# Gates of the gathered experts: one-number indirect transfers in place of a key comparison per slot, compaction ahead of the gate matrix

## The chip, the core and the metric

The kernel runs on one core of a Trainium2 chip. Times are microseconds (us) on the device, of one launch. The engines named below are PE (matrix products), DVE (vector), ACT (activation and copies out of PSUM), POOL (here it issues the indirect transfers) and SP (issues the plain transfers).

## The reference, cut to what matters

One encoder layer over 256 tokens of width 2048: a mixer, a cross attention, and a PEER feed-forward in which every token picks 8 x 16 = 128 of 16384 one-neuron experts. Only the last part is touched:

```python
eid  = (i1 * PEER_N_KEYS + i2).reshape(t, PEER_HEADS * PEER_TOPK)
gate = jax.nn.softmax(top_sc, axis=-1).reshape(t, PEER_HEADS * PEER_TOPK)
u = u_tab[eb]
act = jax.nn.gelu(jnp.einsum('td,tkd->tk', xb, u).astype(jnp.float32))
return jnp.einsum('tk,tkd->td', (gb * act).astype(xb.dtype), v_tab[eb])
```

## The kernel before, in words

The expert tables are rearranged on the host into 128 rows of 128 experts. 104 rows (`RD`) are done densely: products of all their experts with all tokens (the U stage, `u_chunk`, 13 chunks of which the first 6, `LEAD`, run ahead), a multiplication by a gate matrix (`prep`), and products with the second table (the V stage, `v_chunk`, into which the other 7 U chunks are mixed). The experts of the other 24 rows are gathered: each token has at most 40 (`NIT`) of them in slots, and for each slot POOL fetches one row per token (`rows`, 128 x 2048 floats, four buffers in a ring), DVE makes the dot product (`dot`, result `junk`) and later adds the row of the second table times its coefficient (`axpy`, result `hh`). There are 2 token tiles (`tt`) of 128 tokens, 5 blocks of 8 slots each, so 80 dots and 80 axpys.

Every weight of the dense part is loaded as `raw` (128 x 1024, four buffers), rounded by ACT to `hi`, and DVE makes the remainder `lo` (L112, three buffers). PE uses both. A DVE that is late with `lo` stops PE.

`route` (L671) finds the experts and gates of a tile. `gbuild` (L768) writes the gate matrix: for 4 tokens at a time DVE makes two one-hot tiles (L777, L780), ACT scales one (L783), PE multiplies them (`G`, L793), ACT copies the result (L795), and every 16 tokens go to memory (`gd`). `compact` (L753) sorts the gathered slots to the front: five rounds of `pick` (L745, L746) on a key per slot, then `rows_of` (L748) makes the table rows `idx`. The key also holds the slot's place j in its low 7 bits. `weigh` (L891) finds the gates of 8 picked slots: for each slot one comparison of the 128 keys with the picked key, times the masked gates `gsp`, summed along the row (L895).

These side programs are generators. `Weave.pump` takes steps of the first in the list while it has credit, each pump of the main loop adds `rate`, and each `yield` says what a step costs. In `chosen` a block's `weigh` costs 1.8, each dot or axpy 2.2; the rate in the V stage is 1.25 (`RC`). In the sixth U chunk (L848) the rest of `gbuild` is pumped out at once. What this emits is a priority: a list scheduler then sets each engine's order, and each engine works in that fixed order.

Of the kernel before, what the change touches and what calls it, by code (L numbers as in the profile page):

```python
# [21 lines left out]
TT = T // P  # L22
# [11 lines left out]
RD = 104  # L34
# [3 lines left out]
NIT = 40  # L38
# [29 lines left out]
def hybrid_layer_kernel(ctx: ExitStack, tc: tile.TileContext, a: dict, out: bass.AP, dbg=None):  # L68
    nc = tc.nc
# [10 lines left out]
    wv = Weave()  # L80
# [19 lines left out]
    ones = cp.tile([P, P], F32, name="ones")  # L100

# [152 lines left out]
    nc.sync.dma_start(iota, a["iota"])  # L254
    for b in range(1, 8):
        if b == 3:
            wv.add(prep_x())
        col_block(a["w_xyg"], b, xT, xb[:, b, :])
# [409 lines left out]
    i1T, rT, gtT, key, work, gsp, sel, idx = ({} for _ in range(8))  # L668
    flag = cp.tile([P, TT], F32, name="flag")

    def route():  # L671
# [11 lines left out]
        for tt in range(TT):  # L683
# [41 lines left out]
            for j, src in enumerate((i1, rr, gt.rearrange("p h j -> p (h j)"))):  # L725
# [4 lines left out]
            key[tt] = tp.tile([P, P], F32, tag=f"key{tt}", name="key")  # L730
            work[tt] = tp.tile([P, P], F32, tag=f"work{tt}", name="work")
            gsp[tt] = tp.tile([P, P], F32, tag=f"gsp{tt}", name="gsp")
            V.scalar_tensor_tensor(gsp[tt], rr, float(RD), gt.rearrange("p h j -> p (h j)"),
                                   op0=ALU.is_ge, op1=ALU.mult)
            V.tensor_scalar(rr, rr, float(P * P), -float(RD * P * P), op0=ALU.mult, op1=ALU.add)
            V.scalar_tensor_tensor(rr, i1, float(P), rr, op0=ALU.mult, op1=ALU.add)
            V.tensor_tensor(key[tt], rr, iota, op=ALU.add)
            V.tensor_copy(work[tt], key[tt])
# [9 lines left out]
    def rows_of(tt, s):  # L748
        V.tensor_copy(idx[tt][:, s], sel[tt][:, s])
        V.tensor_scalar(idx[tt][:, s].bitcast(U32), idx[tt][:, s].bitcast(U32), 7, None,  # L750
                        op0=ALU.logical_shift_right)

    def compact():  # L753
        for tt in range(TT):
            sel[tt] = tp.tile([P, NIT + 8], F32, tag=f"sel{tt}", name="sel")
            idx[tt] = tp.tile([P, NIT], I32, tag=f"idx{tt}", name="idx")
            for b in range(NB):
                pick(tt, b)
                yield 0.4
            V.max(sel[tt][:, NIT:], work[tt])  # L760
            V.tensor_scalar(flag[:, tt:tt + 1], sel[tt][:, NIT:NIT + 1], 0.0, None, op0=ALU.is_ge)
            rows_of(tt, slice(0, NIT))
            yield 0.6
# [125 lines left out]
    dots, coef, gsel = {}, {}, {}  # L889

    def weigh(tt, b):  # L891
        gsel[tt, b] = tp.tile([P, 8], F32, tag="gsel", name="gsel", bufs=3)
        for k in range(8):
            gj = tp.tile([P, P], F32, tag="gj", name="gj")
            V.scalar_tensor_tensor(gj, key[tt], sel[tt][:, 8 * b + k:8 * b + k + 1], gsp[tt],  # L895
                                   op0=ALU.is_equal, op1=ALU.mult, accum_out=gsel[tt, b][:, k:k + 1])

    def dot(tt, b, k, gat):
        if k == 0:
            dots[tt, b] = tp.tile([P, 8], F32, tag="dots", name="dots", bufs=2)  # L900
        V.scalar_tensor_tensor(junk, gat, 1.0, h[tt], op0=ALU.mult, op1=ALU.mult,  # L901
                               accum_out=dots[tt, b][:, k:k + 1])
        if k == 7:
            c = coef[tt, b] = tp.tile([P, 8], F32, tag="coef", name="coef", bufs=3)
            A.activation(c, dots[tt, b], AF.Gelu_apprx_tanh)
            V.tensor_tensor(c, c, gsel[tt, b], op=ALU.mult)
# [4 lines left out]
    def chosen(blocks):  # L911
# [8 lines left out]
        for n in range(len(tasks) + AHEAD):  # L920
# [11 lines left out]
    def rest():  # L932
# [7 lines left out]
        with tc.If(left > 0):  # L940
            for tt in range(TT):
                for b in range(NB, P // 8):
                    pick(tt, 0)
                    rows_of(tt, slice(0, 8))
# [70 lines left out]
    done.add("pb")  # L1015
    wv.add(gbuild())
    wv.add(compact())
# [53 lines left out]
def _constants():  # L1071
# [13 lines left out]
    return {"cs": np.ascontiguousarray(cs), "md": np.ascontiguousarray(md), "iota": iota,  # L1085
            "ident": np.eye(P, dtype=np.float32)}
# [51 lines left out]
```

## Time and profile before

| | us |
|---|---|
| median of 3 runs | 2260.44 |
| lowest, highest | 2258.86, 2264.28 |
| the profiled execution's own time | 2268.65 |
| its span, first to last instruction | 2266.9 |

| engine | busy us | share of the span |
|---|---|---|
| PE | 2142.0 | 94% |
| DVE | 1812.3 | 80% |
| ACT | 1084.5 | 48% |
| POOL | 397.1 | 18% |

The U stage's first six chunks lie at about 920 to 1260 us, the V stage after that, the last chunk and the output from about 2200 us. PE is busy nearly all the time everywhere but around 1250 us, DVE above all in `route` (900 to 1110 us) and in the V stage. A share is a mean over stages, so what a stage is bound by is read from the stage.

### The profile page before, as it was taken

To read this page: it belongs to the slowest core of one execution; us is meant where nothing else is said; L and a number is where in the kernel's file an instruction comes from. 1 tells how busy PE (TensorE), PEld (TensorE's weight loads), DVE (VectorE), ACT (ScalarE), POOL (GpSimd) and SP (SyncE) were. 2 spreads that over 40 slices of the span, in tenths; PEclk is the share of its full clock that TensorE was granted. 3 is DMA by queue.
4 is the path that set the end of the run, shared out by engine and by line. 5 is a ranking of instruction groups with operands and counts; after the bars stand their busy time and mean duration, and the time that the engine had idled before them with its cause. 6 is when DMAs were issued, how large, how long until landed. Compare 5 with 4: busy or idle time off the path is not lost.

```text
span 2266.9 us, 30039 instructions
## 1 busy us (share of the span) xinstructions
PE 2142.0 (94%) x10830; PEld 1795.0 (79%) x10830; DVE 1812.3 (80%) x2511; ACT 1084.5 (48%) x1639; POOL 397.1 (18%) x218
## 2 busy tenths in 40 slices
PE   8999989999999999999998799999989999898898
PEld 7787878888888888888997577877878777776676
DVE  6748876545544579999978799999989989999985
ACT  6564435444444455545887343434434343443334
POOL 0303120000000000000001222323333232243501
PEclk9999999999999999999999899999999999999999
DMA  8664645565544575556765999977777998876664
GB/s 276 235 211 155 216 132 173 176 191 183 184 141 141 176 241 167 186 179 222 225 200 184 368 343 362 324 250 268 226 283 255 371 336 323 291 267 200 191 212 142
DMA packets 162824, 521.65 MB, mean 230 GB/s; under 512 B 23572, under 2 KB 52756, under 8 KB 149268
## 3 DMA queue, kind: packets, MB, share of 16 engines
q1 hardware_dynamic: 139632, 419.29, 56.2%
q0 software_dynamic: 23040, 100.41, 11.8%
q8 instruction: 85, 1.39, 0.2%
q14 instruction: 67, 0.55, 0.1%
HBM read 569.19 MB, written 17.83 MB: 259 GB/s over the span
## 4 chain that ended last, share of the span: by engine, by line
PE 57%; DVE 15%; issue 12%; DMA 11%; POOL 3%; ACT 2%; POOLq 0%; DVEq 0%; ACTq 0%; SPq 0%
PE U L121 8%; PE wb L121 7%; DVE lo L112 6%; PE xc L160 5%; PE xc L159 5%; PE xc L161 5%; PE U L124 4%; PE wb L124 4%; PE V L860 4%; PE V L861 4%; PE V L859 4%; POOL gat L884 2%; DMA gat<-in_Us_dram,idx 2%; PE G L793 2%; DMA raw<-in_V_dram 2%
## 5 line engine op out<-in xcount | busy, mean ns | idle before, releaser
L111 ACT CAST hi<-raw 128x1024 fp32r<-128x1024 f32 x700 | 734.4, 1050 | 780.5 <-DMA raw<-in_V_dram 255.5
L112 DVE TENSOR_TENSOR lo<-raw,hi 128x1024 fp32r<-128x1024 f32 x700 | 862.0, 1249 | 277.0 <-PE xc L160 140.8
L121 PE MATMUL U<-xn,hi 128*128 128x512 f32 x1664 | 414.2, 397 | 16.4 <-ACT hi L111 16.4
L121 PEld LDWEIGHTS U<-xn,hi 128*128 128x128 f32 x1664 | 308.0, 191 | 75.6 <-ACT hi L111 17.2
L884 POOL DMA_INDIRECT gat<-in_Us_dram,idx x80 | 124.2, 1553 | 1129.1 <-PE U L121 677.3
L124 PE MATMUL U<-xn,lo 128*128 128x256 f32 x1664 | 230.9, 287 | 24.4 <-DVE lo L112 24.1
L860 PE MATMUL V<-lo,ah 128*128 128x512 f32 x560 | 225.7, 403 | 24.2 <-DVE lo L112 23.7
L124 PEld LDWEIGHTS U<-xn,lo 128*128 128x128 f32 x1664 | 217.4, 192 | 38.2 <-DVE lo L112 30.3
L884 POOL DMA_INDIRECT gat<-in_Vs_dram,idx x80 | 185.0, 2312 | 337.1 <-DVE hh L909 304.5
L861 PE MATMUL V<-hi,al 128*128 128x512 f32 x560 | 223.0, 398 | 0.0
L859 PE MATMUL V<-hi,ah 128*128 128x512 f32 x560 | 221.0, 398 | 1.7 <-ACT hi L111 1.5
L901 DVE SCALAR_TENSOR_TENSOR junk<-gat,h 128x2048 f32<-128x2048 f32 x80 | 183.7, 2296 | 14.6 <-DMA gat<-in_Us_dram,idx 14.6
L909 DVE SCALAR_TENSOR_TENSOR hh<-gat,coef,hh 128x2048 f32<-128x2048 f32 x80 | 187.9, 2349 | 5.1 <-DMA gat<-in_Vs_dram,idx 5.1
L860 PEld LDWEIGHTS V<-lo,ah 128*128 128x128 f32 x560 | 106.2, 190 | 59.1 <-DVE lo L112 33.4
L859 PEld LDWEIGHTS V<-hi,ah 128*128 128x128 f32 x560 | 106.1, 189 | 28.8 <-ACT hi L111 2.4
L861 PEld LDWEIGHTS V<-hi,al 128*128 128x128 f32 x560 | 106.2, 190 | 24.9
L860 PE MATMUL V<-lo,xe 128*128 128x512 f32 x256 | 103.1, 403 | 14.1 <-DVE lo L112 14.1
L121 PE MATMUL wb<-hT,hi 128*128 128x512 f32 x448 | 113.9, 398 | 0.7 <-ACT hi L111 0.7
L861 PE MATMUL V<-hi,xe 128*128 128x512 f32 x256 | 101.3, 396 | 0.0
L859 PE MATMUL V<-hi,xe 128*128 128x512 f32 x256 | 96.2, 394 | 3.8 <-ACT hi L111 3.8
L121 PEld LDWEIGHTS wb<-hT,hi 128*128 128x128 f32 x448 | 81.3, 189 | 16.3 <-ACT hi L111 0.9
L121 PE MATMUL wb<-xT,hi 128*128 128x512 f32 x368 | 91.7, 400 | 0.2 <-ACT hi L111 0.2
(330 smaller groups left out, 3234.6 us busy)
## 6 DMA issues: line engine op xcount, KB each, us to landing
raw<-in_U_dram SPq DMA_DIRECT2D x208, 512.0 KB, 4.8
raw<-in_V_dram SPq DMA_DIRECT2D x208, 512.0 KB, 4.4
raw<-in_w_xyg_dram SPq DMA_DIRECT2D x48, 512.0 KB, 4.7
raw<-in_w_qkv_dram SPq DMA_DIRECT2D x48, 512.0 KB, 4.2
raw<-in_w_xk_dram SPq DMA_DIRECT2D x32, 512.0 KB, 4.4
raw<-in_w_xv_dram SPq DMA_DIRECT2D x32, 512.0 KB, 4.4
raw<-in_w_out_dram SPq DMA_DIRECT2D x32, 512.0 KB, 4.0
raw<-in_w_xq_dram SPq DMA_DIRECT2D x32, 512.0 KB, 4.5
```

Source lines behind the costliest of these rows:

```text
L111: A.copy(hi, raw)
L112: V.tensor_tensor(lo, raw, hi.bitcast(F32), op=ALU.subtract)
L121: PE.matmul(pt, hi[:, k * P:(k + 1) * P], xt[:, kb, :], start=(kb == 0), stop=(kb == KB - 1))
L124: PE.matmul(pt[:, :T], lo[:, k * P:(k + 1) * P], xt[:, kb, :T], start=False, stop=False)
L159: PE.matmul(pt, xh, hi[:, w], start=(n == 0), stop=False)
L160: PE.matmul(pt, xh, lo[:, w], start=False, stop=False)
L859: PE.matmul(pt, ah[:, c, t_], hi[:, w], start=(c == 0), stop=False)
L860: PE.matmul(pt, ah[:, c, t_], lo[:, w], start=False, stop=False)
L861: PE.matmul(pt, al[:, c, t_], hi[:, w], start=False, stop=(c == 7))
L884: G.indirect_dma_start(gat, None, a[tab], bass.IndirectOffsetOnAxis(ap=idx[tt][:, k:k + 1], axis=0), bounds_check=NS - 1, oob_is_err=False)
L901: V.scalar_tensor_tensor(junk, gat, 1.0, h[tt], op0=ALU.mult, op1=ALU.mult, accum_out=dots[tt, b][:, k:k + 1])
L909: V.scalar_tensor_tensor(hh[tt], gat, coef[tt, b][:, k:k + 1], hh[tt], op0=ALU.mult, op1=ALU.add)
```

## The change

The gates of a tile are written to memory (`gtd`, 16384 numbers). `compact` is now ahead of `gbuild` in the list. After the five picks, `rows_of` takes the place j from the key's low bits, adds 128 times the token's lane (a new constant `lane`, loaded at the start), and so has an index tile `at` into `gtd`. 40 indirect transfers per tile then fetch one number for each of the 128 tokens into a column of `gsel`. `weigh`, `gsp` and the separate `key` go. In place of the mask in `gsp`, one small operation per block (`g8`) takes the slots with a key of at least 0.

```diff
+    gtd = [dp.tile([P * P, 1], F32, name=f"gtd{tt}") for tt in range(TT)]
...
-            key[tt] = tp.tile([P, P], F32, tag=f"key{tt}", name="key")
+            nc.sync.dma_start(gtd[tt].rearrange("(p j) o -> p (j o)", p=P), gt.rearrange("p h j -> p (h j)"))
...
-            V.scalar_tensor_tensor(gsp[tt], rr, float(RD), gt.rearrange("p h j -> p (h j)"),
-                                   op0=ALU.is_ge, op1=ALU.mult)
...
-            V.tensor_tensor(key[tt], rr, iota, op=ALU.add)
-            V.tensor_copy(work[tt], key[tt])
+            V.tensor_tensor(work[tt], rr, iota, op=ALU.add)
...
     def rows_of(tt, s):
         V.tensor_copy(idx[tt][:, s], sel[tt][:, s])
+        at = tp.tile([P, NIT + 8], I32, tag="at", name="at")[:, s]
+        V.tensor_scalar(at, idx[tt][:, s], P - 1, None, op0=ALU.bitwise_and)
         V.tensor_scalar(idx[tt][:, s].bitcast(U32), idx[tt][:, s].bitcast(U32), 7, None,
                         op0=ALU.logical_shift_right)
+        V.tensor_scalar(at, at, lane, None, op0=ALU.add)
+        for k in range(s.start, s.stop):
+            G.indirect_dma_start(gsel[tt][:, k:k + 1], None, gtd[tt], bass.IndirectOffsetOnAxis(
+                ap=at[:, k - s.start:k - s.start + 1], axis=0), bounds_check=P * P - 1, oob_is_err=False)
+            yield 0.05
...
-            rows_of(tt, slice(0, NIT))
+            gsel[tt] = tp.tile([P, NIT + 8], F32, tag=f"gsel{tt}", name="gsel")
+            yield from rows_of(tt, slice(0, NIT))
...
-    def weigh(tt, b):
-        gsel[tt, b] = tp.tile([P, 8], F32, tag="gsel", name="gsel", bufs=3)
-        for k in range(8):
-            gj = tp.tile([P, P], F32, tag="gj", name="gj")
-            V.scalar_tensor_tensor(gj, key[tt], sel[tt][:, 8 * b + k:8 * b + k + 1], gsp[tt],
-                                   op0=ALU.is_equal, op1=ALU.mult, accum_out=gsel[tt, b][:, k:k + 1])
...
-            V.tensor_tensor(c, c, gsel[tt, b], op=ALU.mult)
+            g8 = tp.tile([P, 8], F32, tag="g8", name="g8")
+            V.scalar_tensor_tensor(g8, sel[tt][:, 8 * b:8 * b + 8], 0.0, gsel[tt][:, 8 * b:8 * b + 8],
+                                   op0=ALU.is_ge, op1=ALU.mult)
+            V.tensor_tensor(c, c, g8, op=ALU.mult)
...
-                if f is dot and k == 0:
-                    weigh(tt, b)
-                    yield 1.8
...
     done.add("pb")
+    wv.add(compact())
     wv.add(gbuild())
-    wv.add(compact())
```

The orders below have no time in them. DVE, the end of the second tile's picks before (the names in brackets are the semaphores that a row waits for; DMASW are those of the indirect transfers, DMAHW of the plain ones):

```order
L745 MAX sel<-work 128x8 [waits DVE_49]
L895 SCALAR_TENSOR_TENSOR gj,gsel<-key,sel,gsp 128x128 [waits DVE_49]
L746 MATCH_REPLACE work<-sel,work 128x128 [waits DVE_49]
L749 CAST idx<-sel 128x40
L895 SCALAR_TENSOR_TENSOR gj,gsel<-key,sel,gsp 128x128 [waits DVE_49]
L112 TENSOR_TENSOR lo<-raw,hi 128x1024 [waits DMAHW1_49,PE_49,Activation_49]
```

and the same place after the change:

```order
L745 MATCH_REPLACE work<-sel,work 128x128 [waits DVE_49]
L748 CAST idx<-sel 128x40
L766 MAX sel<-work 128x8 [waits DVE_49]
L750 TENSOR_SCALAR at<-idx 128x40 [waits DMASW4_49,DMASW3_49,DMASW5_49,DMASW2_49,DMASW6_49,DMASW1_49,DMASW7_49,DMASW0_49,DVE_49]
L767 TENSOR_SCALAR flag<-sel 128x1 [waits DVE_49]
L751 TENSOR_SCALAR idx<-idx 128x40 [waits DVE_49]
L753 TENSOR_SCALAR at<-at,lane 128x40
L113 TENSOR_TENSOR lo<-raw,hi 128x1024 [waits DMAHW2_49,PE_49,Activation_49]
```

The `at` tile has one buffer for both token tiles, so the second tile's `at` row waits for the indirect transfers that read the first tile's; the program's count for each of the eight semaphores there is five transfers, which is all 40, and `lo` rows stand behind it. Between the first tile's last `at` row and this one DVE has 14 `lo` rows.

POOL, its first indirect transfers before:

```order
L884 DMA gat_11170<-in_Us_dram,idx 128x2048
L884 DMA gat_11171<-in_Us_dram,idx 128x2048
L884 DMA gat_11172<-in_Us_dram,idx 128x2048
L884 DMA gat_11173<-in_Us_dram,idx 128x2048
L884 DMA gat_11170<-in_Us_dram,idx 128x2048
```

and after:

```order
L755 DMA gsel<-gtd_6493,at 128x1 x40
L891 DMA gat_11416<-in_Us_dram,idx 128x2048
L891 DMA gat_11417<-in_Us_dram,idx 128x2048
L891 DMA gat_11418<-in_Us_dram,idx 128x2048
L755 DMA gsel<-gtd_6494,at 128x1 x40
L891 DMA gat_11419<-in_Us_dram,idx 128x2048
```

The first tile's 40 stand ahead of all rows of the expert table, the second tile's 40 behind the first three of them.

PE, the end of the gate matrix before (a group of 4 `G` products is 4 tokens):

```order
L124 MATMUL U<-xn,lo 128x256 x2
L793 MATMUL G<-o_10795,o_10793 128x104 x4
L793 MATMUL G<-o_10809,o_10807 128x104 x4
L793 MATMUL G<-o_10824,o_10822 128x104 x4
L793 MATMUL G<-o_10839,o_10837 128x104 x4
L793 MATMUL G<-o_10853,o_10851 128x104 x4
L124 MATMUL U<-xn,lo 128x256 x8
```

and after, the last 11 of its 12 groups that stand without a `U` product between them:

```order
L800 MATMUL G<-o_10986,o_10984 128x104 x4
L800 MATMUL G<-o_11001,o_10999 128x104 x4
L800 MATMUL G<-o_11015,o_11013 128x104 x4
L800 MATMUL G<-o_11029,o_11027 128x104 x4
L800 MATMUL G<-o_11044,o_11042 128x104 x4
L800 MATMUL G<-o_11059,o_11057 128x104 x4
L800 MATMUL G<-o_11073,o_11071 128x104 x4
L800 MATMUL G<-o_11087,o_11085 128x104 x4
L800 MATMUL G<-o_11102,o_11100 128x104 x4
L800 MATMUL G<-o_11117,o_11115 128x104 x4
L800 MATMUL G<-o_11131,o_11129 128x104 x4
L125 MATMUL U<-xn,lo 128x256 x8
```

Seven groups have moved from places among `U` products to this end; the place in the row of `U` products is the same.

## Rows read from the trace of the kernel before

**Rows 1.** Busy us of each engine in five stretches, granted clock, DMA share.

```profile
core 0: us, PE busy (x) PEld busy (x) DVE busy (x) ACT busy (x) POOL busy (x), PEclk, DMA share, GB/s
1047.50:1084.50 37.00, 36.67 (x215) 32.12 (x214) 35.70 (x68) 17.78 (x28) 4.71 (x3) 1.00 0.70 246
1236.00:1260.00 24.00, 4.49 (x16) 3.65 (x16) 14.21 (x12) 4.75 (x9) 7.99 (x4) 0.64 0.99 349
1260.00:1280.00 20.00, 19.71 (x95) 16.64 (x96) 18.61 (x20) 9.98 (x14) 4.82 (x4) 0.92 0.94 353
1300.00:2000.00 700.00, 654.23 (x3171) 539.35 (x3170) 642.45 (x651) 289.96 (x363) 214.90 (x117) 0.99 0.84 303
2000.00:2200.00 200.00, 182.06 (x763) 143.70 (x763) 195.59 (x177) 74.57 (x74) 70.01 (x29) 0.98 0.66 210
```

**Rows 2.** Waits between 1300 and 2200 us: us in total, times, longest.

```profile
PE V L860 <- DVE lo L112: 37.5, 31, 3.7
...
PE U L124 <- DVE lo L112: 20.4, 17, 2.2
```

**Rows 3.** DVE groups, 1200 to 2266 us: busy, mean ns, idle before.

```profile
L895 DVE SCALAR_TENSOR_TENSOR gj<-key,sel,gsp 128x128 f32<-128x128 f32 x56 | 19.4, 347 | 0.0
...
L895 DVE DVE_READ_ACCUMULATOR gj<-key,sel,gsp 128x1 f32 x56 | 4.6, 82 | 0.0
...
L906 DVE TENSOR_TENSOR coef<-coef,gsel 128x8 f32<-128x8 f32 x10 | 1.6, 162 | 0.0
```

**Rows 4.** Timeline of POOL, its first gathers: start, us taken, idle before.

```profile
1061.94 1.16 POOL L884 DMA_INDIRECT gat<-in_Us_dram,idx  x1 [673.28 <-PE U L121]
1067.07 1.74 POOL L884 DMA_INDIRECT gat<-in_Us_dram,idx  x1 [3.97 <-PE U L121]
1082.53 1.82 POOL L884 DMA_INDIRECT gat<-in_Us_dram,idx  x1 [13.73 <-DVE sel L745]
1238.25 2.00 POOL L884 DMA_INDIRECT gat<-in_Us_dram,idx  x1 [153.90 <-DVE gat L1031]
```

**Rows 5.** DVE groups, 1047.5 to 1084.5 us.

```profile
L112 DVE TENSOR_TENSOR lo<-raw,hi 128x1024 fp32r<-128x1024 f32 x13 | 15.5, 1209 | 0.0
L1031 DVE MEMSET gat<- 128x2048 f32 x3 | 5.3, 1765 | 1.1 <-issue 1.1
```

**Rows 6.** Instructions of line 884: ns min/median/max.

```profile
L884 POOL DMA_INDIRECT gat<-in_Us_dram,idx x80: 984/1670/4308, 1061.9 to 2115.3; - x80
...
DMA to landing us min/median/max: 2.1/7.4/10.3
```

**Rows 7.** Timeline of DVE, then of POOL, around 1980 us.

```profile
1979.45 2.23 DVE L811 TENSOR_TENSOR act<-raw,act 128x1024 f32<-128x1024 f32 x1
1981.59 2.35 DVE L112 TENSOR_TENSOR lo<-raw,hi 128x1024 fp32r<-128x1024 f32 x2
1983.86 2.29 DVE L901 SCALAR_TENSOR_TENSOR junk<-gat,h 128x2048 f32<-128x2048 f32 x1
...
1987.21 0.68 DVE L873 TENSOR_TENSOR hh<-hh,V 128x512 f32<-128x512 f32 x1
...
1979.80 8.35 POOL L884 DMA_INDIRECT gat<-in_Vs_dram,idx  x1 [4.69 <-DVE hh L909]
1988.46 1.44 POOL L884 DMA_INDIRECT gat<-in_Us_dram,idx  x1 [0.30 <-issue]
```

**Rows 8.** Timeline of PE, last groups of G.

```profile
1229.97 1.29 PE L793 MATMUL G<-o,o 128*128 128x104 f32 x8 [0.32 <-ACT o L783]
...
1234.44 1.28 PE L793 MATMUL G<-o,o 128*128 128x104 f32 x8 [0.20 <-ACT o L783]
```

**Rows 9.** Chain of waits, 1195 to 1290 us: start, us, what.

```profile
1199.30 1.77 PE G L793 x16
...
1236.29 11.39 DMA gd<-gs
...
1247.77 8.43 DMA raw<-gd
```

More of the change, by code (lines that the diff above doesn't have):

```diff
@@ L100, in hybrid_layer_kernel @@
     ones = cp.tile([P, P], F32, name="ones")
+    lane = cp.tile([P, 1], F32, name="lane")
     def raw_tile(src):
@@ L254, in hybrid_layer_kernel @@
     nc.sync.dma_start(iota, a["iota"])
+    nc.sync.dma_start(lane, a["lane"])
     for b in range(1, 8):
@@ L666, in top16 @@
                 V.match_replace(src, vals[:, rs], src, -3.0e38)
-    i1T, rT, gtT, key, work, gsp, sel, idx = ({} for _ in range(8))
+    i1T, rT, gtT, work, sel, idx, gsel = ({} for _ in range(7))
+    gtd = [dp.tile([P * P, 1], F32, name=f"gtd{tt}") for tt in range(TT)]
     flag = cp.tile([P, TT], F32, name="flag")
@@ L729, in route @@
             i1T[tt], rT[tt], gtT[tt] = trio[:, 0], trio[:, 1], trio[:, 2]
-            key[tt] = tp.tile([P, P], F32, tag=f"key{tt}", name="key")
+            nc.sync.dma_start(gtd[tt].rearrange("(p j) o -> p (j o)", p=P), gt.rearrange("p h j -> p (h j)"))
             work[tt] = tp.tile([P, P], F32, tag=f"work{tt}", name="work")
-            gsp[tt] = tp.tile([P, P], F32, tag=f"gsp{tt}", name="gsp")
-            V.scalar_tensor_tensor(gsp[tt], rr, float(RD), gt.rearrange("p h j -> p (h j)"),
-                                   op0=ALU.is_ge, op1=ALU.mult)
             V.tensor_scalar(rr, rr, float(P * P), -float(RD * P * P), op0=ALU.mult, op1=ALU.add)
             V.scalar_tensor_tensor(rr, i1, float(P), rr, op0=ALU.mult, op1=ALU.add)
-            V.tensor_tensor(key[tt], rr, iota, op=ALU.add)
-            V.tensor_copy(work[tt], key[tt])
+            V.tensor_tensor(work[tt], rr, iota, op=ALU.add)
             yield 2.5
@@ L888, in hybrid_layer_kernel @@
     turn = [0]
-    dots, coef, gsel = {}, {}, {}
-    def weigh(tt, b):
-        gsel[tt, b] = tp.tile([P, 8], F32, tag="gsel", name="gsel", bufs=3)
-        for k in range(8):
-            gj = tp.tile([P, P], F32, tag="gj", name="gj")
-            V.scalar_tensor_tensor(gj, key[tt], sel[tt][:, 8 * b + k:8 * b + k + 1], gsp[tt],
-                                   op0=ALU.is_equal, op1=ALU.mult, accum_out=gsel[tt, b][:, k:k + 1])
+    dots, coef = {}, {}
     def dot(tt, b, k, gat):
@@ L943, in rest @@
                     pick(tt, 0)
-                    rows_of(tt, slice(0, 8))
+                    for _ in rows_of(tt, slice(0, 8)):
+                        pass
                     for _ in chosen([(tt, 0)]):
@@ L1085, in _constants @@
     return {"cs": np.ascontiguousarray(cs), "md": np.ascontiguousarray(md), "iota": iota,
+            "lane": np.arange(P, dtype=np.float32).reshape(P, 1) * P,
             "ident": np.eye(P, dtype=np.float32)}
```

## The prediction

> **What bounds the kernel now.** Read first the table of busy time by stretch [rows 1]: its rows give, for each stretch, how long each engine worked. From 1047.5 to 1084.5 us, in the U stage, PE works 36.67 of 37.00 us and DVE 35.70: both are full, PE sets the pace, and DVE only just keeps up. From 1236 to 1260 us PE works 4.49 of 24 us. That gap is not an engine's: the chain of waits shows the last piece of the gate matrix written to memory in 11.39 us and read back in 8.43 us [rows 9]. From 1300 to 2200 us PE works 654.23 + 182.06 = 836 of 900 us and DVE 642.45 + 195.59 = 838. Read next what PE waits for there [rows 2]: of its 64 idle us, 37.5 + 20.4 = 57.9 ended with a `lo` from DVE. So in the V stage less DVE work can help, in the U stage it cannot, and whatever stops DVE in the U stage stops PE. POOL's timeline [rows 4] says where POOL is free: its first row of the expert table is issued at 1061.94 us, and between the third and the fourth it sits idle for 153.90 us.
>
> **What goes.** 80 comparisons of a slot. After 1200 us there are 56, at 347 ns and 82 ns for reading the sum [rows 3]: 19.4 + 4.6 = 24.0 us of DVE. The other 24 (80 less 56) lie before 1200 us, in the U stage, where PE is the bound: nothing. The mask `gsp` and the copy of the key go there too: nothing. What comes in the V stage is ten operations on 128x8, priced like the one that is there already, 162 ns [rows 3]: 1.6 us. DVE is relieved of 22.4 us.
>
> How much of that PE gets back is read from the pumps. The V stage has 12 chunks of 16 pumps with V and 7 chunks of 16 with U, 304 in about 940 us, 3.1 us each. Ten times 1.8 credits at 1.25 a pump are 14.4 pumps: the gathered part ends about 45 us earlier, while before that it goes on at nearly the old density. In the last stretch [rows 1] PE idles 200 - 182.06 = 18 of 200 us, 9%; free of gathered work those 45 us give 4 us, and I add 1 us for the comparisons that no longer stand between `lo` rows. Taken: 5 us. The bounds are 0 (each `lo` waits for something else next, a load or ACT) and 22 us (all of it returns).
>
> **What comes: 80 transfers of one number, and a wait.** On SP the two stores of the gates and the load of `lane` go in among hundreds of loads of 512 KB; nothing. On POOL the second tile's 40 fit into the 153.90 us that it is idle [rows 4], even at 2.35 us each, and the three table rows that they are queued with are not used before the fourth buffer is cleared, just ahead of 1238.25 us. On POOL, then, nothing is lost. The price is on DVE. In the order after the change, the second tile's `at` row waits for all 40 transfers of the first tile, and the `lo` rows of the U stage stand behind it.
>
> *When does DVE come to that row?* The old trace has nearly the same work from 1047.5 to 1084.5 us: 13 `lo` and the three clearings of ring buffers [rows 5] in 37 us. The new order has 14 `lo` between the two `at` rows, one more at 1.2 us: 38 us.
>
> *How many transfers are through by then?* No transfer of one number is in the trace; the nearest rows are the table rows, which also carry one index for each of 128 tokens. POOL takes at least 984 ns for one [rows 6], and 0.30 us pass between two that wait for nothing [rows 7]: 1.28 us, the lower bound. It can take far longer. The one at 1979.80 us took 8.35 us [rows 7]: in this time DVE ran a product of `act`, remainders and a dot, each of which reads two operands from SBUF, back to back, and the transfer ended 0.94 us after DVE began L873, which has one operand in PSUM. So such DVE work holds the transfer up, and 0.98 us is what it takes after. The three in the U stage took 1.16, 1.74 and 1.82 us [rows 4]; their mean and the gap are 1.87 us, and this is what I take while DVE runs, since they ran beside this very work. In 38 us 20 transfers are through. The upper bound is 2.35 us, two `lo` rows [rows 7].
>
> The page "SBUF — State Buffer" of the Trainium skill (its box on DVE blocking a DMA of GpSimd) names DVE's two-port modes, as in a plain copy, as what starves such a transfer, and leaves the impression that remainders and products would not. By that alone the transfers would come at 1.28 us and the stall below would be 15 us, not 28; the row of 8.35 us speaks against it, and the same page's section "Who interferes with whom" does have the case of two SBUF operands.
>
> *How long does DVE stand?* Once it waits, nothing holds POOL up: the other 20 take 20 x 1.28 = 25.6 us, and the last needs at least 2.1 us to land [rows 6]: 28 us. With 1.28 us all along it is 40 x 1.28 + 2.1 - 38 = 15 us, with 2.35 us all along 94 + 2.1 - 38 = 58 us.
>
> The page "DMA: Bandwidth & Descriptors" of the Trainium skill (anatomy of a DMA from GpSimd) gives about 2.0 us of fixed cost to each such transfer; one after the other that would be an estimate of 80 - 38 = 42 us. It puts most of it down to the landing, and the landings here overlap, since up to eight transfers are under way; the 1.44 us of the row at 1988.46 us [rows 7] is already below it.
>
> *What does PE lose?* A half block takes PE 37/13 = 2.85 us. With three `lo` buffers DVE may be one or two halves ahead; I take one and a half, 4 us (bounds 0 and 8.5). So 28 - 4 = 24 us, bounds 7 and 58. After a pause PE restarts slowly: in the 24 us about the old gap the granted clock is 0.64, and in the 20 us after it 0.92 [rows 1], so 8% of 20 us, 2 us.
>
> **What moves.** Seven groups of the gate matrix go from between U products to the end of `gbuild`. At the end a group takes (1234.44 - 1229.97)/3 = 1.49 us [rows 8], set by ACT, so 10.4 us come. Where they stood PE was the bound, and two groups (16 recorded products) took 1.77 us [rows 9], so 7 x 0.885 = 6.2 us go. Plus 4 us (bounds 0 and 10). The write and the read of 11.39 and 8.43 us stand behind the end as before.
>
> **The sum.** 24 + 2 + 4 - 5 = +25 us. The profiled execution took 2268.65 us, which becomes 2293.65; it is 8 us above the median of the runs and 4 us above the highest, so I put the 25 us on the median: 2260.44 + 25 = 2285 us, slower by 1.1%.
>
> **The rivals.** (1) *The wait is hidden and the V stage pays in full.* The transfers go at 1.28 us although DVE is busy, the stall is 15 us, PE is three halves behind and loses 7; the clock costs 1, the gate matrix 4, and all 22 us come back: 7 + 1 + 4 - 22 = -10, 2250 us, faster. It decides as soon as more than 12 us of DVE time return as PE time. For it: 57.9 us of PE's waits name `lo` [rows 2]. Against it: the row of 8.35 us, and that the freed time lies in the last 45 us. (2) *They cancel.* The short wait, 15 - 4 = 11, with 1 for the clock, none for the gate matrix and 12 of the 22 back: 0, 2260 us. (3) *The transfers are slow throughout:* 2.35 us each even while DVE stands, because the loads on the same DMA engines hold them (their busy share is 0.70 there [rows 1]): 58 - 4 + 2 + 4 - 5 = +55, 2315 us. For it: landings of up to 10.3 us [rows 6]. Against it: these move four bytes per token, not 8 KB. (4) *The wait isn't real,* that is, POOL is through the 40 before DVE comes there: 38/40 = 0.95 us each would be needed, below the shortest of 80 rows, so this has no chance of its own.
>
> **How the numbers follow.** Forecast 0.68 (its own range 2268 to 2305), rival 3 0.10, rival 2 0.11, rival 1 0.11. Within 0.3%, 6.8 us, a measurement of this kernel can hardly tell a change from none. Rival 1 is faster, rival 2 the same, the others slower: 0.11, 0.11, 0.78. The bounds of all terms give 7 + 1 + 0 - 22 = -14 and 58 + 2 + 10 - 0 = +70, 2246 to 2330 us; leaving out the two ends, where every term would have to fall to its bound at once, the range is 2255 to 2318 us.
>
> **What would show it.** In the new profile the second tile's `at` row should have DVE idle before it for 15 to 58 us, at about 1085 us, ended by a transfer into `gsel`, and PE idle at the same time by some 4 us less. POOL's rows into `gsel` should stand nearly 2 us apart before that wait and 1.3 us apart in it. The lone groups of `G` should be 12 at 1.49 us, and the stretch from there to the first V product as long as it was. In the V stage PE's waits for `lo` should fall by about 5 us, with the last `hh` some 45 us earlier against the end. The prediction is wrong if DVE hardly stands at that row, or if the V stage shortens by more than 12 us.

## The result, and the profile after the change

The changed kernel took 2287.77 us (median of 4 runs, 2278.66 to 2296.71), the kernel before, with a run beside it, 2261.77 us (2258.86 to 2264.28, 4 runs): the ratio is 1.0123, 95% interval 1.0099 to 1.0147. Forecast were 2285 us, slower by 1.1%. The profiled execution of the change took 2296.71 us, the highest of its four, with a span of 2294.9 us: 28.0 above the span before, where the medians stand 26.0 apart. A run more than 1.5% above the fastest of its kernel counts as slow; among all runs here that holds only for five of the six of the first experiment and three of the six of the second.

DVE's timeline around the `at` rows of the two tiles (start us, us, what; in brackets the idle time ahead of a row and what ended it):

```profile
1045.42 0.20 DVE L750 TENSOR_SCALAR at<-idx 128x40 int32<-128x40 int32 x1
...
1049.07 0.27 DVE L753 TENSOR_SCALAR at<-at,lane 128x40 int32<-128x40 int32 x1
...
1088.42 0.29 DVE L766 MAX8 sel<-work 128x8 f32<-128x128 f32 x1
1114.11 0.19 DVE L750 TENSOR_SCALAR at<-idx 128x40 int32<-128x40 int32 x1 [25.39 <-DMA gsel<-gtd,at]
```

The transfers need the first tile's last `at` row, at 1049.07 us. DVE comes to the second tile's row at 1114.11 - 25.39 = 1088.72 us, 39.6 us after that, and then stands for 25.39 us, until the last transfer of the first tile has landed. PE's timeline behind it:

```profile
1089.22 3.82 PE L122 MATMUL U<-xn,hi 128*128 128x512 f32 x16
1092.88 1.11 PE L125 MATMUL U<-xn,lo 128*128 128x256 f32 x8
1115.85 2.08 PE L125 MATMUL U<-xn,lo 128*128 128x256 f32 x8 [21.86 <-DVE lo L113]
1117.73 3.62 PE L122 MATMUL U<-xn,hi 128*128 128x512 f32 x8
```

PE runs on for some 5 us on what DVE had made ahead, idles 21.86 us, and then takes 2.08 us for eight products with `lo` that took 1.11 before, and 3.62 for eight with `hi`, of which sixteen took 3.82. POOL's timeline, from the first transfer to the last of the first tile:

```profile
1050.31 4.97 POOL L755 DMA_INDIRECT gsel<-gtd,at  x1 [658.81 <-DVE foldu L853]
...
1083.55 1.77 POOL L755 DMA_INDIRECT gsel<-gtd,at  x1 [0.31 <-issue]
...
1088.25 1.00 POOL L755 DMA_INDIRECT gsel<-gtd,at  x1 [0.31 <-issue]
...
1111.66 0.99 POOL L755 DMA_INDIRECT gsel<-gtd,at  x1 [0.30 <-issue]
```

The one at 1088.25 is the 22nd: 21 transfers went out in 37.9 us while DVE worked, 1.81 us each on average, the other 19 from there to 1111.66 us, while it stood, 1.30 us apart. The average hides a spread: the first and the third took 4.97 and 3.72 us, and half of the 21 stand at most 1.52 us from the next. The transfers of both tiles by their line, and their landing:

```profile
L755 POOL DMA_INDIRECT gsel<-gtd,at x80: 992/1006/4967, 1050.3 to 1180.0; - x80
...
DMA to landing us min/median/max: 2.3/4.3/9.5
```

Busy time by stretch, columns as in [rows 1]:

```profile
1047.50:1084.50 37.00, 36.07 (x212) 31.83 (x211) 35.58 (x54) 19.63 (x35) 28.71 (x19) 1.00 0.62 199
1088.50:1114.00 25.50, 5.49 (x32) 4.64 (x30) 0.22 (x1) 1.42 (x3) 19.66 (x20) 0.69 0.04 10
1116.90:1126.30 9.40, 9.40 (x46) 8.13 (x46) 5.23 (x8) 3.94 (x9) 7.20 (x7) 0.74 1.00 404
1116.00:1136.00 20.00, 20.00 (x116) 18.07 (x117) 13.29 (x19) 13.10 (x32) 14.94 (x14) 0.85 0.86 329
1300.00:2000.00 700.00, 659.98 (x3199) 543.83 (x3198) 643.81 (x576) 289.95 (x367) 220.36 (x125) 0.99 0.86 312
2000.00:2200.00 200.00, 180.91 (x757) 142.54 (x756) 189.50 (x159) 74.53 (x74) 58.50 (x27) 0.98 0.64 205
```

In the third of these stretches the first seven transfers of the second tile go out, 1.34 us apart, while the DMA engines are full (1.00) and DVE works 5.23 of 9.40 us. So it is not the loads that slow POOL's transfers in the first stretch (DMA share 0.62), and the difference that is left in these rows is a DVE that works without gaps.

The gate matrix's last groups on PE, and the chain of waits behind them:

```profile
1250.26 1.29 PE L800 MATMUL G<-o,o 128*128 128x104 f32 x8 [0.20 <-ACT o L790]
...
1266.68 1.28 PE L800 MATMUL G<-o,o 128*128 128x104 f32 x8 [0.21 <-ACT o L790]
```

```profile
1268.60 11.07 DMA gd<-gs
1279.72 8.47 DMA raw<-gd
```

These are 12 groups, (1266.68 - 1250.26)/11 = 1.49 us apart, and the write and read stand behind them as in [rows 9]. What PE waits for between 1300 and 2200 us, to be read beside [rows 2]:

```profile
PE V L867 <- DVE lo L113: 35.8, 29, 3.6
...
PE U L125 <- DVE lo L113: 12.3, 16, 2.1
```

Together 48.1 us, where 57.9 stood. The last rows of `hh`, before and after:

```profile
L909 DVE SCALAR_TENSOR_TENSOR hh<-gat,coef,hh x80: 2336/2346/2375, 1327.4 to 2185.9; 128x2048 f32<-128x2048 f32 x80
```

```profile
L912 DVE SCALAR_TENSOR_TENSOR hh<-gat,coef,hh x80: 2326/2348/2407, 1349.5 to 2169.9; 128x2048 f32<-128x2048 f32 x80
```

That is 81 us before the end, and 125. **Where the 28 us lie:** the gate matrix ends at 1266.68 + 1.28 = 1267.96 us, before at 1234.44 + 1.28 = 1235.72 [rows 8], 32.2 us later; from there to the end it is 2294.9 - 1267.96 = 1026.9 us, before 2266.9 - 1235.72 = 1031.2, 4.2 us shorter. In this pair of profiles the loss lies ahead of the gate matrix's end, in the U stage, and the gain behind it, in the V stage. The size of the gain is known less well than one pair shows: in the seven other traces of this change's V stage, those of the runs below with transfers ahead of it, the part behind the gate matrix takes 1018.7 to 1028.0 us, 3 to 12.5 us less than in the one trace of the kernel before.

### The profile page after: what moved, and what is told of

Read it like the earlier page. It is cut to its first block, busy times and chain, and to the rows that moved or that the text cites. A ratio compares the mean times of both kernels' runs of the same rounds, so it can differ in the third digit from the quotient of the medians.

```text
span 2294.9 us, 30100 instructions
## 1 busy us (share of the span) xinstructions
PE 2150.8 (94%) x10830; PEld 1801.3 (78%) x10830; DVE 1795.8 (78%) x2361; ACT 1084.4 (47%) x1639; POOL 481.5 (21%) x298
## 4 chain that ended last, share of the span: by engine, by line
PE 57%; DVE 19%; DMA 12%; issue 7%; ACT 3%; POOL 2%; DVEq 0%; ACTq 0%; POOLq 0%; SPq 0%
DVE lo L113 8%; PE wb L122 7%; PE U L122 6%; PE xc L161 5%; PE xc L162 5%; PE xc L160 5%; PE V L867 5%; PE V L868 5%; PE V L866 5%; DMA raw<-in_V_dram 4%; PE wb L125 4%; PE U L125 3%; DMA raw<-in_U_dram 3%; DVE hh L912 2%; PE G L800 2%
## 5 line engine op out<-in xcount | busy, mean ns | idle before, releaser
L122 PE MATMUL U<-xn,hi 128*128 128x512 f32 x1664 | 419.1, 399 | 21.3 <-ACT hi L112 21.3
L125 PE MATMUL U<-xn,lo 128*128 128x256 f32 x1664 | 230.9, 287 | 37.9 <-DVE lo L113 37.9
L755 POOL DMA_INDIRECT gsel<-gtd,at x80 | 101.9, 1274 | 684.0 <-DVE foldu L853 658.8
L891 POOL DMA_INDIRECT gat<-in_Vs_dram,idx x80 | 169.3, 2117 | 352.0 <-DVE hh L912 329.3
```

The costliest lines, as they stand in the source:

```text
L122: PE.matmul(pt, hi[:, k * P:(k + 1) * P], xt[:, kb, :], start=(kb == 0), stop=(kb == KB - 1))
L125: PE.matmul(pt[:, :T], lo[:, k * P:(k + 1) * P], xt[:, kb, :T], start=False, stop=False)
L891: G.indirect_dma_start(gat, None, a[tab], bass.IndirectOffsetOnAxis(ap=idx[tt][:, k:k + 1], axis=0), bounds_check=NS - 1, oob_is_err=False)
```

## The experiments

All twelve stand here. Each was timed beside the kernel before on its chip, whose medians lay between 2260 and 2264 us.

### Two `at` tiles, so that nothing waits

```diff
-        at = tp.tile([P, NIT + 8], I32, tag="at", name="at")[:, s]
+        at = tp.tile([P, NIT + 8], I32, tag="at", name="at", bufs=2)[:, s]
```

> The change with a second buffer for the tile `at`, and nothing else: every engine's order in the U and V stages is that of the change. Theory (the loss is the wait of the second tile's `at` row): the 25.4 us for which DVE stood and the 21.9 us that PE stood behind it are gone, and the some 3 us in which PE restarted slowly; 2288 - 25 = 2263 us, 2257 to 2269, and it stays a few us above the kernel before, by the gate matrix less the V stage (+7 - 4). Rival A (the transfers cost by being there: they slow DVE's rows or the loads, and the wait only names them): 2278 us or more. Rival B (the wait moves on to the first `g8` or to the expert rows queued behind the 80 transfers, and PE loses as much there): 2280 us or more, with a PE wait of over 10 us between 1085 and 1250 us.

Measured: 2330.39 us median of six; five took 2327.77 to 2339.49 us, 40 to 52 us more than the change, and one 2277.18, 10.6 us less. The wait was gone, and five runs of six were slower. PE's timeline of the slowest of them (of the one at 2277.18 us there is no trace):

```profile
1099.35 1.03 PE L800 MATMUL G<-o,o 128*128 128x104 f32 x8
...
1139.11 2.04 PE L800 MATMUL G<-o,o 128*128 128x104 f32 x8 [22.92 <-issue]
...
1148.76 0.37 PE L125 MATMUL U<-xn,lo 128*128 128x256 f32 x1 [2.52 <-issue]
1151.59 0.37 PE L125 MATMUL U<-xn,lo 128*128 128x256 f32 x1 [2.46 <-issue]
```

From ACT's timeline, its second copy of `G`:

```profile
1121.36 0.51 ACT L802 COPY gs<-G 128x416 f32<-128x416 f32 x1 [11.68 <-remote]
```

and the busy time of the stretch, columns as in [rows 1]:

```profile
1120.00:1180.00 60.00, 13.22 (x41) 10.61 (x42) 7.44 (x12) 7.74 (x21) 38.04 (x38) 0.53 0.15 50
```

PE starts a product every 2.8 us and waits for nothing that the trace shows ("issue"). ACT's second copy of `G` starts at 1121.36 us, after 11.68 us without work; the products of the second group had ended at 1099.35 + 1.03 = 1100.38, 21 us before. Loads stop too: between 1116.30 and 1162.01 us SP issues none, and the load of 1162.01 us goes out as a `lo` ends. All this while POOL issues transfers 1.30 us apart. So neither the theory's 2263 us nor rival A's reason (slowed DVE rows, queued loads: a `lo` there takes 1.23 us as ever, and the DMA engines are busy for a share of 0.15) nor rival B's (a wait that moves on) explains these five runs. There is a **hold-up** that the change's trace does not show. What it needs was open.

### Two `at` tiles, and the gate matrix not pushed back

```diff
-        at = tp.tile([P, NIT + 8], I32, tag="at", name="at")[:, s]
+        at = tp.tile([P, NIT + 8], I32, tag="at", name="at", bufs=2)[:, s]
...
-            yield 0.05
+            yield 0.001
```

and likewise 0.001 for the compaction's yields of 0.4 and 0.6.

> As the run with two `at` buffers, and the compaction's steps cost the weave almost nothing (0.001 each where they cost 9.2 credits in all), so that the gate matrix is not pushed back: 5 groups stand alone at its end, as before the change, and not 12. Theory (7 groups moved to the end cost 1.49 us each and give back 0.885 each, 4 us by that, and up to the 7.5 us that the two profiles leave for it): 4 to 7.5 us below the run with two buffers alone, so 2256 to 2259 us, and 2 to 5 us below the kernel before, which is the V stage's gain alone. Rival (PE is full in the U stage, so a group costs the same wherever it stands): no difference to two buffers alone, 2263 us.

Measured: 2309.75 us median of six, from 2269.41 to 2334.67. The hold-up again, to a different extent from run to run: in the run that was traced (2298.10 us) PE works 45.56 of the 60 us from 1120 to 1180 us. It covers what the run was to tell; the run with this edit alone, below, tells it.

### The kernel before, without the comparisons

```diff
-        for k in range(8):
-            gj = tp.tile([P, P], F32, tag="gj", name="gj")
-            V.scalar_tensor_tensor(gj, key[tt], sel[tt][:, 8 * b + k:8 * b + k + 1], gsp[tt],
-                                   op0=ALU.is_equal, op1=ALU.mult, accum_out=gsel[tt, b][:, k:k + 1])
+        V.scalar_tensor_tensor(gsel[tt, b], sel[tt][:, 8 * b:8 * b + 8], 0.0, gsp[tt][:, 8 * b:8 * b + 8],
+                               op0=ALU.is_ge, op1=ALU.mult)
...
-                    yield 1.8
```

> The kernel before, with the 80 comparisons left out and nothing in their place but one operation on 128x8 per block: the gates of the picked slots are not looked up, so the coefficients are others; everything else is computed. It measures what the freed 22 us of DVE are worth in the V stage alone, with no transfer, no new wait and the gate matrix where it was. Theory (the gathered part only ends some 45 us earlier, and little of that comes back): 4 to 5 us, 2257 us, 2253 to 2260. Rival 1 of the prediction (each us of DVE comes back as a us of PE): 2261 - 22 = 2239 us. Rival that each `lo` waits for something else next: 2261 us.

Measured: 2259.61 us (2256.51 to 2266.18, 6 runs), ratio 0.9987, 0.9965 to 1.0010: some 3 us, not to be told from nothing, and far from 22. PE's waits between 1300 and 2200 us:

```profile
PE V L860 <- DVE lo L112: 34.4, 29, 3.9
PE U L124 <- DVE lo L112: 11.9, 14, 2.1
```

46.3 us where 57.9 stood [rows 2]: of 24 us that DVE is freed of, PE sees 12 fewer in its waits for `lo`, and the time 3.

### Each transfer of the first tile twice

```diff
-        for k in range(s.start, s.stop):
+        for k in [k for k in range(s.start, s.stop) for _ in range(2 if s.stop == NIT and tt == 0 else 1)]:
...
-            yield 0.05
+            yield 0.025 if s.stop == NIT and tt == 0 else 0.05
```

> The change with each of the first tile's 40 transfers issued twice. Theory (the wait is POOL's pace: all transfers of the first tile at some 1.3 us each once DVE stands): DVE stands 40 x 1.30 = 52 us longer, some 77 us, and PE with it; 2288 + 52 = 2340 us, 2332 to 2350. Rival (the wait is set by the landing of a transfer or by another event, and the transfers overlap): DVE stands about as long as now, 2288 to 2300 us.

Measured: 2395.24 us (2389.50 to 2402.07, 4 runs), ratio 1.0587, 1.0556 to 1.0618: 107 us above the change, twice what was expected. DVE's wait at the second tile's row, and PE's timeline behind it:

```profile
1163.35 0.18 DVE L750 TENSOR_SCALAR at<-idx 128x40 int32<-128x40 int32 x1 [55.87 <-DMA gsel<-gtd,at]
```

```profile
1125.93 0.58 PE L122 MATMUL U<-xn,hi 128*128 128x512 f32 x1 [2.22 <-issue]
1128.73 0.58 PE L122 MATMUL U<-xn,hi 128*128 128x512 f32 x1 [2.22 <-issue]
...
1223.23 0.33 PE L800 MATMUL G<-o,o 128*128 128x104 f32 x1 [1.77 <-issue]
```

The wait grew with the number of transfers, from 25.39 to 55.87 us, which refutes the rival, but not to the 77 us that were expected: the first `g8` waits 10.5 us ahead of it, so DVE comes to the row later, and another 8.54 us of idle DVE lie before a `lo` that stands ahead of the row here. And the hold-up set in as well, from about 1102 us on, and lasted some 8 us beyond POOL's last transfer of the run, which went out at 1218.46 us. A product (its weight load and itself) takes 2.80 us, two instructions at 1.40.

### Only the gate matrix not pushed back

The change with one `at` tile, and

```diff
-            yield 0.05
+            yield 0.001
...
-                yield 0.4
+                yield 0.001
...
-            yield 0.6
+            yield 0.001
```

> The change with one buffer for `at` as it is, and the compaction's steps at 0.001 credit each, so that 5 groups of the gate matrix stand alone at its end instead of 12. The wait of the second tile's `at` row stays. Theory (the seven groups cost 4 us by the prediction's rows, up to 7.5 us by the two profiles: 32.3 us between the ends of the gate matrix less 21.9 of PE's pause and 2.9 of its slow restart): 2288 - 4 to 2288 - 7.5, 2280 to 2284 us, with DVE standing 25 us as before. Rival (PE is full there, a group costs the same wherever it stands): 2288 us.

Measured: 2281.87 us (2279.05 to 2295.26, 5 runs), ratio 1.0103, 1.0070 to 1.0136: 5.9 us below the change by the medians. But the runs of the two kernels cover the same range (2278.66 to 2296.71 there), so the times alone do not rule out the rival, nothing. The trace says more. PE's pause in place of the one for `lo`, and its last group of `G`:

```profile
1119.57 2.04 PE L800 MATMUL G<-o,o 128*128 128x104 f32 x8 [22.88 <-ACT o L790]
...
1263.56 1.28 PE L800 MATMUL G<-o,o 128*128 128x104 f32 x8 [0.20 <-ACT o L790]
```

DVE's wait stays; the product that PE stops at is another, since groups of `G` now stand there. The pause is 1.0 us longer than in the change and the gate matrix ends 1266.68 - 1263.56 = 3.1 us earlier: some 4 us for the seven groups, in one pair of traces.

### Additions on POOL, two `at` tiles

Three attempts at a run without the wait and without the hold-up. In the first an addition was meant to stand behind each transfer:

```diff
...
+            if s.stop == NIT:
+                G.tensor_tensor(pad, pad, pad, op=ALU.add)
             yield 0.05
...
```

> The change with two `at` buffers, and one addition of 128x256 on POOL behind each transfer, so that transfers stand at least 2.3 us apart and not 1.3. It tells why two buffers alone gave 2330 and not 2263 us. New theory (a run of transfers 1.3 us apart holds up the other engines: in the run with two buffers PE starts one instruction per 1.4 us from 1144 to 1173 us with nothing to wait for, and its releases reach DVE and ACT up to 15 us late; with pauses between transfers that does not set in): 2263 us, 2257 to 2270, steady from run to run, and less than 5 us of PE's idle time in the U stage without a releaser. Rival (each transfer costs the others a fixed time, whatever its distance from the next, or the loads queue behind them): 2290 us or more, with PE idle as in the run with two buffers.

Measured: 2275.70 us (2269.09 to 2287.59, 8 runs), ratio 1.0056, 1.0031 to 1.0082. The scheduler had put all 80 additions ahead of the transfers, which then stood as close as ever but began 14 us later. From POOL's timeline:

```profile
959.63 41.70 POOL L759 TENSOR_TENSOR pad<-pad 128x256 f32<-128x256 f32 x40
1064.17 1.18 POOL L756 DMA_INDIRECT gsel<-gtd,at  x1 [62.84 <-DVE at L754]
```

Its stretches, and under them those of the kernel before:

```profile
900.00:1047.00 147.00, 134.53 (x756) 116.32 (x755) 145.25 (x412) 67.24 (x106) 77.09 (x81) 0.99 0.52 161
1120.00:1180.00 60.00, 59.94 (x404) 54.84 (x403) 44.94 (x66) 52.07 (x136) 48.72 (x38) 1.00 0.81 256
```

```profile
900.00:1047.00 147.00, 144.43 (x841) 127.45 (x841) 146.50 (x432) 78.08 (x122) 0.00 (x0) 1.00 0.55 181
...
1120.00:1180.00 60.00, 60.00 (x412) 55.33 (x411) 44.07 (x64) 52.86 (x138) 0.00 (x0) 1.00 0.69 208
1180.00:1236.00 56.00, 54.79 (x384) 50.35 (x383) 43.52 (x67) 50.87 (x151) 0.00 (x0) 1.00 0.54 164
```

No wait, no hold-up: PE works 59.94 of 60 us beside 38 transfers. The additions cost it 144.43 - 134.53 = 9.9 us before 1047 us, where DVE is full. Without them it would be, by this estimate, some 2275.7 - 9.9 = 2266 us, 22 below the change: near the theory's 2263. The rival (a fixed cost for each transfer) falls, and so does the new theory's half: pauses between transfers are not needed.

In the second the additions depend on the index tile and do stand between the transfers:

```diff
...
+        if s.stop == NIT:
+            pad = tp.tile([P, 256], F32, tag="pad", name="pad")
+            G.memset(pad, 0.0)
+            G.tensor_copy(pad[:, :NIT], at)
...
+            if s.stop == NIT:
+                G.tensor_tensor(pad, pad, pad, op=ALU.add)
             yield 0.05
```

> The change with two `at` buffers, and on POOL between any two transfers one addition of 128x256 that depends on the index tile, so that it now does stand between them (in the earlier run of this kind the 80 additions ran ahead of all transfers). Transfers are 2.3 us apart or more; the additions take about 1 us each of the way that DVE and POOL share. Theory (long runs of transfers 1.3 us apart set off the hold-up of PE): the U stage has no PE idle time without a releaser, 2260 to 2275 us, at most 15 us from run to run. Rival (the hold-up needs only many transfers beside a DVE that pauses): runs above 2300 us as with two buffers alone.

Measured: 2284.94 us (2280.75 to 2289.51, 5 runs), ratio 1.0110, 1.0091 to 1.0128. No hold-up in five runs, but above the theory's 2260 to 2275: the additions take 0.62 to 1.64 us each, DVE works 56.79 us from 1120 to 1180 us where it worked 44.94 in the run before, and PE works 33.12 us of the 37 from 1047 to 1084 us. That the additions delay DVE and so PE is the reading that fits this; no run tests it alone. The transfers by their line:

```profile
L759 POOL DMA_INDIRECT gsel<-gtd,at x80: 1014/1192/4961, 1049.2 to 1244.2; - x80
```

They start no later than with two `at` tiles alone (1049.35 us), and stand (1244.2 - 1049.2)/79 = 2.47 us apart. So it is not a later start that kept the hold-up away here; whether it is the spacing or a DVE that the additions keep busy, this run does not tell.

In the third only the start is later: a chain of 14 additions ahead of the first transfer.

```diff
...
+        if s.stop == NIT and tt == 0:
+            pad = tp.tile([P, 256], I32, tag="pad", name="pad")
+            G.memset(pad, 0)
+            G.tensor_tensor(pad[:, :NIT], at, at, op=ALU.subtract)
+            for _ in range(14):
+                G.tensor_tensor(pad, pad, pad, op=ALU.add)
+            at2 = tp.tile([P, NIT], I32, tag="at2", name="at2")
+            G.tensor_tensor(at2, at, pad[:, :NIT], op=ALU.add)
+            at = at2
```

> The change with two `at` buffers, and ahead of the first tile's transfers a chain of 14 additions of 128x256 on POOL, on which they depend, so that the 80 transfers start some 14 us later than with two buffers alone, as they did in the run where the 80 additions ran ahead (there without a hold-up, in eight runs); DVE is not slowed before 1047 us this time. The first `g8` may now wait for the first eight transfers, up to 9 us. Theory (the wait of the `at` row cost the change 22 us of PE and some 3 us of slow restart, and the hold-up is set off only if transfers run beside a DVE that has caught up early): 2288 - 25 = 2263 us, up to 2272 with the wait of `g8`, and no PE idle time without a releaser. Rival (the hold-up comes whenever the wait is gone; that it did not come in the earlier run was owed to the slower DVE before 1047 us): 2300 us or more in most runs.

Measured: 2273.52 us (2270.90 to 2285.55, 6 runs), ratio 1.0070, 1.0048 to 1.0092: 14 us below the change, no hold-up in six runs. The wait of the first `g8`, and the stretch with it:

```profile
1075.97 0.17 DVE L916 SCALAR_TENSOR_TENSOR g<-sel,gsel 128x8 f32<-128x8 f32 x1 [4.89 <-DMA gsel<-gtd,at]
```

```profile
1047.00:1084.00 37.00, 28.47 (x155) 24.58 (x154) 30.35 (x38) 15.81 (x29) 31.16 (x28) 0.94 0.50 148
```

PE loses 37 - 28.47 = 8.5 us there, which the expectation had up to 9, and in the change 37 - 36.07 = 0.9. So 14.3 + 8.5 - 0.9 = 21.9 us is what the `at` wait had cost. The 8.5 us are not the wait of `g8` alone: beside the additions two `lo` rows take 3.19 us, where they took 2.38 in the change, and PE waits 2.4 us for `lo` there. That the hold-up comes whenever the wait is gone is refuted; what in the later start (1061.22 us, with two `at` tiles alone 1049.35) decides is open.

### The transfers among the table rows

Compaction behind the gate matrix again, `at` and the `gsel` tiles apart, and in `chosen`:

```diff
...
+    def gate(tt, k):
+        if k % 8 == 0:
+            gsel[tt, k // 8] = tp.tile([P, 8], F32, tag="gsel", name="gsel", bufs=2)
+        G.indirect_dma_start(gsel[tt, k // 8][:, k % 8:k % 8 + 1], None, gtd[tt], bass.IndirectOffsetOnAxis(
+            ap=at_of[tt][:, k:k + 1], axis=0), bounds_check=P * P - 1, oob_is_err=False)
...
                 held.append(rows(tab, tt, 8 * b + k))
+                if f is dot:
+                    gate(tt, 8 * b + k)
```

> Compaction behind the gate matrix again, an `at` tile for each token tile, and each transfer of a gate issued behind its slot's table row, into a tile of 8 with two buffers: 24 transfers go out in the U stage, beside a DVE that is full, and the other 56 in the V stage, at most 4 in a row. Theory (no wait in the U stage, no long run of transfers, the gate matrix as before the change, and the V stage gains what the run without comparisons showed, 3 us): 2258 us, 2253 to 2262. Rival (short runs of transfers hold PE up too, or they delay the table rows): above 2268 us.

Measured: 2302.26 us (2295.38 to 2306.91, 6 runs), ratio 1.0180, 1.0154 to 1.0206: the rival. The first `g8` waits 8.9 us, and the V stage is slower. Its stretch from 1360 to 2000 us, and under it that of the kernel before:

```profile
1360.00:2000.00 640.00, 589.89 (x2824) 487.89 (x2823) 569.29 (x506) 254.07 (x324) 285.99 (x167) 0.97 0.83 295
```

```profile
1360.00:2000.00 640.00, 600.23 (x2897) 494.30 (x2897) 587.29 (x604) 264.17 (x331) 199.42 (x108) 0.98 0.84 299
```

POOL is busy 87 us longer, DVE 18 and PE 10 us less: each gate's transfer takes POOL nearly as long as a whole table row (medians 1.42 and 1.67 us), and between 1300 and 2200 us DVE waits 29.0 us for table rows, before 19.7. That this is what makes the V stage slower is not shown: PE's waits for `lo` there add up to 50.1 us, less than the 57.9 before.

The same at a lower rate:

```diff
-RA, RB, RC = 1.1, 1.9, 1.25
+RA, RB, RC = 1.1, 1.9, 1.19
```

> As the run before, with the rate of the gathered work in the V stage at 1.19 in place of 1.25, so that it ends as near the end as before the change and DVE is less dense all along. Theory (little came back because the freed DVE time lay in the last 45 us; spread, more of the 22 us returns as PE's waits for `lo`): 5 to 12 us below the run with 1.25, 2246 to 2253 us. Rival (PE's waits for `lo` come from loads and ACT, so it does not matter where the freed time lies): the same as with 1.25, 2258 us.

Measured: 2292.50 us (2288.22 to 2303.37, 6 runs), ratio 1.0152, 1.0124 to 1.0181. The 9.8 us below the run before are the size expected, at a time 40 us above the one expected. In a kernel whose table rows are late they don't prove the reason; the next two runs do.

### The comparisons kept, and moved into the U stage

The kernel before with

```diff
-        gsel[tt, b] = tp.tile([P, 8], F32, tag="gsel", name="gsel", bufs=3)
+        gsel[tt, b] = tp.tile([P, 8], F32, tag="gsel", name="gsel", bufs=10)
```

> The kernel before with ten buffers in place of three for the gates of a block (`gsel`), nothing else: nothing is fetched, the 80 comparisons stay, but the order can now put all of them into the U stage, between the 345th and the 377th `lo` (some 1085 to 1180 us), where 24 stood before; in the two windows behind 1120 us there DVE works 44 of 60 and 43.5 of 56 us. The steps keep their credit, so the gathered part ends where it did. Theory (the comparisons are free where DVE has gaps, and the V stage is freed of 24 us of DVE, evenly): 2263 - 3 to 2263 - 12, 2251 to 2260 us. Rival 1 (DVE is late in the U stage by the 56 comparisons that came, 24 us of work in a stage that PE paces): no gain or slower, 2261 to 2275 us.

Measured: 2253.72 us (2242.24 to 2261.68, 12 runs), ratio 0.9964, 0.9947 to 0.9981: faster than the kernel before by 8.4 us and than the change by 34. Its stretches:

```profile
1120.00:1180.00 60.00, 60.00 (x410) 55.25 (x409) 57.50 (x145) 52.17 (x136) 0.00 (x0) 1.00 0.71 209
1180.00:1236.00 56.00, 56.00 (x397) 51.90 (x395) 49.17 (x99) 50.90 (x147) 0.00 (x0) 1.00 0.53 167
```

DVE works 57.50 us of 60 where it worked 44.07, and PE still 60 of 60: the comparisons are free there. And without the credit for them:

```diff
                     weigh(tt, b)
-                    yield 1.8
```

> As the run before, without the credit of 1.8 for each block's comparisons, so that the gathered part ends 16 `lo` rows earlier, as it does in the change. Theory of the prediction (the freed time then lies in the last 45 us and little of it comes back): 2 to 7 us above the run before. Rival (where the freed time lies does not matter): the same.

Measured: 2260.33 us (2254.53 to 2272.43, 12 runs), ratio 1.0000, 0.9981 to 1.0020: 6.6 us above the run before, as the theory has it. The last rows of `hh`, in the run before (span 2256.1) and here (2257.1):

```profile
L909 DVE SCALAR_TENSOR_TENSOR hh<-gat,coef,hh x80: 2329/2348/2373, 1331.6 to 2175.1; 128x2048 f32<-128x2048 f32 x80
```

```profile
L909 DVE SCALAR_TENSOR_TENSOR hh<-gat,coef,hh x80: 2331/2347/2400, 1312.1 to 2132.4; 128x2048 f32<-128x2048 f32 x80
```

81 us against 125 us before the end. The same DVE time is worth 8 us where it is taken out evenly and about 2, not to be told from nothing, where it lies at the end.

## Why the prediction was right, step by step

- **When DVE comes to the row:** forecast 38 us for the 14 `lo` behind the first tile's last `at` row, measured 39.6. POOL began 1.2 us after that row, so the transfers had 38.4.
- **How many transfers are through:** forecast 20 at 1.87 us, measured 21 at 1.81. As an average the value taken from the three table rows beside the same DVE work was right, with some luck: two long transfers among the first three lift it, and the middle one of the 21 stands 1.52 us from the next. The lower bound, 1.28, is what they take when DVE stands (1.30 measured). The page "SBUF — State Buffer" of the Trainium skill, by its box alone, would have had 1.28 all along and 15 us; the 1.81 us beside DVE's work and the wait of 25.39 us are against that. Its section "Who interferes with whom" has two operands in SBUF contend with a GpSimd instruction that reads SBUF, but infers that they leave a transfer's descriptors alone; here the first transfer took 4.97 us beside a DVE that ran nothing but rows of two operands until 1054 us. Whether its descriptors waited or the reading of its indices, no run tells.
- **How long DVE stands:** forecast 28 us, measured 25.39. The page "DMA: Bandwidth & Descriptors" of the Trainium skill and its fixed 2.0 us per transfer, one after the other, would have been 42 by the prediction's estimate: landings overlap, as the 1.30 us between issues show beside at least 2.3 us to land.
- **What PE loses:** forecast 28 - 4 = 24 us and 2 for the clock, measured 21.86 us of pause and about 3 for the restart (0.97 and 1.7 us on the two rows of PE behind it, and some tenths on the next, at a granted clock of 0.85 from 1116 to 1136 us). By runs: 22 us (additions ahead) and 21.9 us (later start), each with what PE loses elsewhere in it added back from its trace. That this wait is the loss is shown by the rows of the two pauses and by these two runs, not by the first run made for it.
- **The gate matrix:** 12 groups at 1.49 us as forecast; the seven that moved were forecast at 4 us, bounds 0 and 10. The run that put them back gives some 4 us by its trace and 5.9 by the medians, which alone can't be told from nothing.
- **The V stage:** forecast -5, bounds 0 and -22. The profiles give -4.2 (the other traces, -3 to -12.5), the run without comparisons -3, the run with dense early comparisons -2; the last two can't be told from 0, and 22 is out. PE's waits for `lo` fell by 9.8 us where about 5 were forecast, and, as in the run without comparisons (11.6 and 3), not all of that came back as time. That the gathered part ends some 45 us earlier held: the last `hh` stands 125 us before the end and before 81.
- **The sum:** 24 + 2 + 4 - 5 = 25, measured 26.0 by the medians, with an interval of 22 to 33 us by the ratio. That the two meet within 1 us is luck, since the terms are off by 1 to 3 us each; their mechanisms and rough sizes held.
- **The rivals.** Rival 1 (short wait, all of 22 us back) fails at both halves: 25.39 us, and 2 to 4. Rival 2 needed the short wait too, and 12 us back. Rival 3 needed 2.35 us per transfer even while DVE stands; it is 1.30, and 1.34 in the stretch with full DMA engines. Rival 4 had no chance, and the wait was real.
- **What the prediction did not see:** that the wait is not the only price of a long run of transfers. It treated DVE as the one engine that a transfer could touch. In the change itself this costs nothing, as no row of PE's U stage there is without a releaser; with the wait taken away it made five runs of six 40 to 52 us slower than the change.

## What to carry to other kernels

Price a new wait by what is queued behind it on its engine, and count its releases: here 40 transfers, half of them not through, stood ahead of the `lo` rows that PE lives on. Many small indirect transfers were dear in every place tried here, and no run with them was faster than the kernel before by its median: each takes POOL at least as long as a row of 8 KB (992 and 984 ns). A comparison of 0.35 us on DVE, moved to a stage where DVE has gaps, beat them by one changed buffer count. And work taken from an engine pays where that engine is waited for: the same 24 us were worth 8 us spread out and 2, if anything, at the end.

## What the runs showed that was not expected

- **A hold-up of PE by a run of transfers.** With 80 transfers in a row, those behind 1099 us 1.30 us apart, and a DVE that had caught up, PE started one instruction per 1.40 us with nothing to wait for, and ACT copied a finished product 21 us late, as long as POOL issued. By their times it came in five of six runs with two `at` tiles, in five of the six of their variant and in all four with doubled transfers, and a trace of each shows it; not in the change, and not in the 19 runs in which the transfers began 12 to 15 us later or stood 2.47 us apart. Perhaps it keeps itself up, since a DVE that is fed nothing does not slow POOL; no run tests that. Through what POOL holds up the other engines, and what sets it off, stays open.
- **POOL's additions slow a full DVE.** 80 of 128x256 ahead of the transfers cost PE 9.9 us in a stage where DVE works 145 of 147 us; in the run with the later start, two `lo` rows beside such additions took 3.19 us in place of 2.38.
- **A transfer of one number costs POOL no less than one of 8 KB a token:** 992 ns at least, against 984 [rows 6].
